# Shift and scale of the first two channel tiles loaded tile by tile, and squares summed on TensorE, in the first projection of a hybrid block

## The chip, the cores and the metric

The kernel runs on one core of a Trainium2 chip. The metric is device microseconds (us) of one execution; a time is the median of several runs. The engines are TensorE (PE, with PEld for its weight loads), VectorE (DVE), ScalarE (ACT), GpSimd (POOL) and SyncE (SP), which here issues nearly all loads.

## The reference, cut to what matters

One layer of a diffusion backbone: a latent stream x of 512 tokens and a context stream of 256 tokens, both 2048 channels wide. The change lies in the first steps, up to the projection of the first heads:

```python
mod = (c_act @ w_mod + b_mod)[:, None, :]          # c_act = silu(c)
mod_c = (cc_act @ w_mod + b_mod)[None, None, :]
sh1, sc1, gt1, sh2, sc2, gt2 = jnp.split(mod, 6, axis=-1)
csh1, csc1, cgt1, csh2, csc2, cgt2 = jnp.split(mod_c, 6, axis=-1)
h = rmsnorm(x, g_norm1) * (1 + sc1) + sh1
hc = rmsnorm(ctx, g_norm1) * (1 + csc1) + csh1
lat_in, lat_gates = project_heads(h, w_in, gla_w_lr, gla_b_lr, mlstm_b_gate)
ctx_in, ctx_gates = project_heads(hc, w_in, gla_w_lr, gla_b_lr, mlstm_b_gate)
...
x = x + gt1 * merge_groups(lat_gla, lat_ml, lat_gates[0], lat_gates[1],
                           gla_g_norm, mlstm_g_norm, w_out, x.dtype)
h2 = rmsnorm(x, g_norm2) * (1 + sc2) + sh2
x = x + gt2 * conv_ffn(h2, rows, GRID_W, w_up, conv_w, conv_b, w_down)
```

Everything is float32. Behind the projection come two scans in both directions, an output projection, an MLP with a 3x3 convolution and a last norm.

## The kernel before, in words

Activations stand transposed: a channel tile is 128 channels by 512 latent tokens (`xl[k]`, 16 tiles, 256 KB each) or by 256 context tokens (`xc[k]`, loaded in pairs). Products of the layer split both operands into a high part of type fp32r and a low part and sum three matmuls (`mm3`): ScalarE casts the high part (`split`, a CAST), VectorE subtracts it for the low part. The norm's sums and the shift and scale sums run in plain float32.

`project_first` computes the projections of heads 0 and 1 together, as the weights of the adaLN shift and scale still come in. Stage kp covers the two channel tiles 2 kp and 2 kp + 1, with a weight of 512 KB per head (`raw_h`). A head has six groups: two of x with a moving operand of 512 tokens (g = 0, 1), two of x with tokens on the output's partitions (g = 2, 3), two of the context stream (g = 4, 5). Head 0 accumulates over all stages in six PSUM banks (`banks`, tag acc). Head 1 sums each stage in a bank of its own (tag psb, two buffers) and is moved to SBUF (`sums`, tiles `e`), by ScalarE in stage 0 and by an add on VectorE later (`early_group`; `early_pair` does g = 0 and 1 of stage 0 at once).

What stands before the first product: `stream_rstd` squares the 16 x tiles on ScalarE, adds them up on VectorE, sums over channels with one matmul against ones (`ss_l`) and takes the root (`mean_rsqrt`, result `rl`). `mod_load` loads the shift or scale weights of two channel tiles (four tiles `raw_m` of 512 KB), `mod_rows` sums them in 16 matmuls (`ps_m`) and copies them out on ScalarE, `mod_cols` turns them into columns (two small matmuls) that VectorE puts into `scol` (region 1, scale) or `shcol` (region 0, shift). `modulate` multiplies tiles with the root, applies scale and shift, and splits them into `hTh` and `hTl` (x) or `hch` and `hcl` (context). The context stream has its own norm (`ss_c`, `rc`) while the first x products run. Eight matmuls of ones and `rl` without a use of their own precede the first product.

The order on PE is the program's (`pinned`); on the other engines a scheduler sets it from priorities, and `tc.issue_after` and `behind` hold an instruction behind a named one of its engine. Loads go through one queue of SP, in program order; each issue waits for the landing of the load eight places ahead, and for its buffer (`mraw`, seven; `wraw`, four).

Of the kernel before, what the change touches and what calls it, by code (L numbers as in the profile page):

```python
# [18 lines left out]
P = 128  # L19
# [27 lines left out]
C_END = C_ONE + 1  # L47


def constants():  # L50
# [7 lines left out]
    c[:, C_ONE] = 1.0  # L58
    return c
# [11 lines left out]
def block_kernel(ctx: ExitStack, tc: tile.TileContext, a: dict, out: bass.AP):  # L71
# [43 lines left out]
    cols = keep.tile([P, 148], F32, name="cols")  # L115
# [160 lines left out]

    def mod_cols(region, n, bank, rows):

        pc = bank[:, 256:260].rearrange("p (b c) -> p b c", c=2)
        for b in range(2):  # L280
            mm(pc[:, b, :], rows[:, P * b : P * b + P], cc(C_SA, 2), start=True, stop=True)
        with tc.high_priority():
            for b in range(2):
                k = 2 * n + b
                if region == 1:
                    V.tensor_scalar(out=scol[:, k, :], in0=pc[:, b, :], scalar1=bp1[:, k : k + 1],
                                    scalar2=gn1[:, k : k + 1], op0=ALU.add, op1=ALU.mult)
                else:
                    V.tensor_scalar(out=shcol[:, k, :], in0=pc[:, b, :], scalar1=bmod[:, k : k + 1],
                                    scalar2=None, op0=ALU.add)  # L290
# [105 lines left out]
    def early_pair(w, sums):  # L396

        (wh, wl), ps = w, [psb(f"a1_0_{g}", BANKS[g]) for g in range(2)]
        for n, (ws, xs) in enumerate(((wh, hx[0]), (wl, hx[0]), (wh, hx[1]))):
            for k in range(2):  # L400
                for g in range(2):
                    mm(ps[g], ws[:, k, P * g : P * g + P], xs[k], start=(n == 0 and k == 0), stop=(n == 2 and k == 1))
        for g in range(2):
            sums[g] = actp.tile(list(BANKS[g]), F32, name=f"e0_{g}", tag=f"ah{KT - 4 + g}")
            with tc.high_priority():
                S.activation(sums[g], ps[g], AF.Copy, scale=SCALE if g == 0 else 1.0)  # L406

    def project_first():

        banks = [acc(f"a0_{g}", BANKS[g]) for g in range(6)]  # L410
        sums = [None] * 4 + [accp.tile([P, DK + DV], F32, name=f"e0_{4 + j}", tag=f"sum{j}") for j in range(CJ)]
        stream_rstd(xl, rl, "l", T)
        for r in (1, 0):
            mod_cols(r, 0, *mod_rows(r, 0, mod_load(r, 0)))
        w1, w0 = (load_split(a["w_heads"][h, 0], f"h{h}_0") for h in (1, 0))
# [3 lines left out]
        with tc.high_priority():  # L419
# [1023 lines left out]
```

## Time and profile before

| what | value |
|---|---|
| time, median of 3 runs | 2513.3 us (2512.97 to 2513.51) |
| the profiled execution's own time | 2511.87 us |
| its span | 2510.1 us |
| PE busy | 2469.3 us, 98% |
| VectorE, ScalarE busy | 1815.0 us (72%), 1024.0 us (41%) |
| share of PE in the chain that ended last | 85% |
| the stage kp = 0, which the change touches | from the start to the first product of kp = 1 at 55.45 us |
| loads | 385 GB/s in the first fortieth of the span, 415 GB/s from 50 to 60 us |

A row of the timeline gives start, duration, engine, line, operation, output<-inputs, form and count, and in brackets the idle time before it with what ended that. A row of the chain gives start, duration and what the chain ran through. A row of a stretch gives its bounds, its length, each engine's busy time with its instructions, the granted TensorE clock, the DMA engines' share and GB/s. An operation of PE in float32 shows as two records.

### The profile page before, as it was taken

Reading aid. Unit: us, or ns where it says so; the run is one execution under the profiler, and the core shown is the slowest. Engines: PE = TensorE matmul, PEld = TensorE weight load, DVE = VectorE, ACT = ScalarE, POOL = GpSimd, SP = SyncE. Lnnn points to the kernel's source line nnn. Section 1 sums busy time; section 2 is a strip of 40 time slices with the busy share of each in tenths; the row PEclk is TensorE's granted clock in tenths of the full one; section 3 lists DMA queues with packets and bytes.
Section 4 is the critical chain, followed back from the end, with each engine's and each line's share of the span. In section 5 each row is a group of like instructions: output and inputs, shape, how many; then the busy total and the mean of one; then the engine's idle time right before and its main releaser. Section 6 shows DMA issues by size and latency. Waiting matters only on the chain.

```text
span 2510.1 us, 39398 instructions
## 1 busy us (share of the span) xinstructions
PE 2469.3 (98%) x15740; PEld 2204.1 (88%) x15740; DVE 1815.0 (72%) x2880; ACT 1024.0 (41%) x1517; POOL 182.5 (7%) x242
## 2 busy tenths in 40 slices
PE   6999999999999999999999999999999999999998
PEld 4887889888987888888989999999999999999997
DVE  6666754554445877858988787878787878787886
ACT  4224543332213233226454444444444444444445
POOL 0000000000000000000020101010101010101022
PEclk9999999999999999999999999999999999999999
DMA  9741011123334878842373737373636363646464
GB/s 385 271 172 42 26 43 51 51 76 125 110 117 155 286 274 304 299 158 99 108 176 101 168 104 166 107 168 104 167 104 166 107 162 108 161 113 160 113 186 135
DMA packets 121552, 372.20 MB, mean 148 GB/s; under 512 B 13908, under 2 KB 18328, under 8 KB 121368
## 3 DMA queue, kind: packets, MB, share of 16 engines
q1 hardware_dynamic: 94680, 318.29, 37.7%
q0 software_dynamic: 25600, 50.34, 11.4%
q8 instruction: 123, 2.02, 0.3%
q10 hardware_dynamic: 1088, 1.05, 0.1%
q14 instruction: 61, 0.50, 0.1%
HBM read 319.30 MB, written 50.33 MB: 147 GB/s over the span
## 4 chain that ended last, share of the span: by engine, by line
PE 85%; issue 9%; DVE 2%; DMA 2%; POOL 1%; ACT 1%; SPq 0%; DVEq 0%; POOLq 0%; ACTq 0%
PE a L98 19%; PE dn L98 17%; PE uv L98 15%; PE ug L98 14%; PE ga L98 7%; PE po L98 4%; PE wo L98 3%; PE sl L98 1%; PE ps_m L98 1%; DMA raw_m<-in_w_mod 1%; PE cst L98 1%; PE s L98 1%; DMA xl<-in_xT 0%; POOL x2d L1269 0%; DMA x2d<-st 0%
## 5 line engine op out<-in xcount | busy, mean ns | idle before, releaser
L98 PE MATMUL dn<-gh,lo_d 128*128 128x512 f32 x672 | 262.3, 390 | 0.3 <-DVE lo_d L93 0.3
L98 PE MATMUL dn<-gh,hi_d 128*128 128x512 f32 x672 | 261.6, 389 | 0.0
L98 PE MATMUL dn<-gl,hi_d 128*128 128x512 f32 x672 | 261.6, 389 | 0.0
L1215 DVE SCALAR_TENSOR_TENSOR cv<-pads,cwt,cv 128x512 f32<-128x512 f32 x344 | 239.5, 748 | 0.6
L1269 POOL DMA_DIRECT2D x2d<-st x160 | 140.1, 928 | 1142.7 <-ACT st L1268 1057.5
L313 DVE SCALAR_TENSOR_TENSOR sum_m<-raw_m,csil,sum_m 128x512 f32<-128x512 f32 x240 | 180.1, 750 | 9.0 <-DMA raw_m<-in_w_mod 3.1
L93 DVE TENSOR_TENSOR lo_buv<-sum_uv,hi_buv 128x1024 fp32r<-128x1024 f32 x80 | 98.0, 1224 | 103.6 <-ACT hi_buv L92 103.6
L98 PEld LDWEIGHTS dn<-gh,lo_d 128*128 128x128 f32 x672 | 126.1, 188 | 28.9 <-DVE lo_d L93 2.6
L98 PE MATMUL a<-hi_h,hTh 128*128 128x256 f32 x512 | 150.4, 294 | 0.5 <-ACT e L406 0.5
L98 PEld LDWEIGHTS dn<-gl,hi_d 128*128 128x128 f32 x672 | 126.2, 188 | 25.9
L98 PEld LDWEIGHTS dn<-gh,hi_d 128*128 128x128 f32 x672 | 126.2, 188 | 25.6
L98 PE MATMUL a<-hi_h,hTl 128*128 128x256 f32 x512 | 144.7, 283 | 0.0
L98 PE MATMUL a<-lo_h,hTh 128*128 128x256 f32 x512 | 144.7, 283 | 0.0
L92 ACT CAST hi_d<-raw_d 128x1024 fp32r<-128x1024 f32 x86 | 88.6, 1030 | 131.9 <-PE ug L98 70.6
L93 DVE TENSOR_TENSOR lo_d<-raw_d,hi_d 128x1024 fp32r<-128x1024 f32 x86 | 102.9, 1196 | 48.1 <-ACT hi_d L92 47.5
L98 PE MATMUL ug<-bth,hi_bug 128*128 128x256 f32 x480 | 136.7, 285 | 0.1
L98 PE MATMUL uv<-bth,lo_buv 128*128 128x256 f32 x480 | 135.9, 283 | 0.8 <-DVE lo_buv L93 0.8
L98 PE MATMUL uv<-bqh,lo_auv 128*128 128x256 f32 x480 | 135.9, 283 | 0.0
L98 PE MATMUL uv<-bth,hi_buv 128*128 128x256 f32 x480 | 135.9, 283 | 0.0
L98 PE MATMUL uv<-bql,hi_auv 128*128 128x256 f32 x480 | 135.8, 283 | 0.0
L98 PE MATMUL ug<-bqh,lo_aug 128*128 128x256 f32 x480 | 135.8, 283 | 0.0
L98 PE MATMUL uv<-btl,hi_buv 128*128 128x256 f32 x480 | 135.8, 283 | 0.0
(379 smaller groups left out, 7347.2 us busy)
## 6 DMA issues: line engine op xcount, KB each, us to landing
raw_m<-in_w_mod SPq DMA_DIRECT2D x192, 512.0 KB, 5.2
raw_d<-in_w_down SPq DMA_DIRECT2D x82, 512.0 KB, 3.4
raw_ug<-in_w_up SPq DMA_DIRECT2D x80, 512.0 KB, 3.5
x2d<-st POOLq DMA_DIRECT2D x160, 256.0 KB, 5.5
raw_uv<-in_w_up SPq DMA_DIRECT2D x80, 512.0 KB, 6.2
raw_h<-in_w_heads SPq DMA_DIRECT2D x64, 512.0 KB, 3.6
raw_ga<-in_w_gates SPq DMA_DIRECT2D x32, 512.0 KB, 4.5
raw_wo<-in_w_out SPq DMA_DIRECT2D x32, 512.0 KB, 4.8
```

The lines of the kernel that those rows point to most:

```text
L92: cast[0] = S.copy(hi, x).ins
L93: return V.tensor_tensor(out=lo, in0=x, in1=hi.bitcast(F32), op=ALU.subtract).ins
L98: ins = PE.matmul(*args, **kw)
L313: V.scalar_tensor_tensor(out=parts[0], in0=x, scalar=ck, in1=parts[0], op0=ALU.mult, op1=ALU.add)
L1215: V.scalar_tensor_tensor(out=t3, in0=src, scalar=w, in1=t3, op0=ALU.mult, op1=ALU.add)
L1269: nc.gpsimd.dma_start(x2d[k], t, accum_op=ALU.add)
```

## The change

Four things change, all in the stage kp = 0 and a little of kp = 1.

- The small inputs `cols` and `cvec` become columns of `consts` and come with it in one load instead of three.
- The squares of x are no longer added in one chain: each goes into a tile of its own, VectorE adds pairs, and eight matmuls sum the pairs on PE. Of the context's squares VectorE now computes every other one, the adds stay.
- Shift and scale of tiles 0 and 1 are loaded tile by tile (`mod_half_load`, two loads of 512 KB for a tile and a region; the host's layout of `w_mod1` follows), summed (`mod_half_rows`, 16 matmuls of 128 columns) and applied tile by tile. The order of loads is: head weight 1, tile 0's four, head weight 0, tile 1's four, then context and the next shift and scale as before.
- `first_groups` multiplies tile 0 into six banks (head 1's g = 0 to 3, head 0's g = 0 and 1), then tile 1 into the same. Head 1's four banks are moved out together; head 0's g = 2 and 3 follow, then `ss_c`, the scale of tiles 2 and 3, the context groups, and the shift of tiles 2 and 3. Tile 4's and 5's scale and shift move from stage 0 into stage 1.

```diff
-    cols = keep.tile([P, 148], F32, name="cols")
+    cols, cv = cst[:, C_COLS:C_CV], cst[:, C_CV:]
...
-    def early_pair(w, sums):
...
+    def mod_half_load(region, b):
+
+        raws = []
+        for q in range(2):
+            raws.append((wraw if b and q else mraw).tile([P, 4, 256], F32, name=f"raw_mh{region}_{b}_{q}", tag="raw"))
+            nc.sync.dma_start(raws[q], a["w_mod1"][8 * region, 2 * b + q])
+        return [raw.rearrange("p a (c n) -> p (a c) n", n=P) for raw in raws]
+
+    def mod_half_rows(region, b, raws):
+
+        bank = psb(f"ps_mh{region}_{b}")
+        for q in range(2):
+            for g in range(8):
+                r = 32 * (g % 4)
+                mm(bank[r : r + 32, 0:P], cact[:, 8 * q + g, :], raws[q][:, g, :], start=(q == 0 and g < 4),
+                   stop=(q == 1 and g >= 4), skip_group_check=True)
+        rows = tmp.tile([P, 256], F32, name=f"rows_mh{region}_{b}", tag="rows")[:, 0:P]
+        with tc.high_priority():
+            S.copy(rows, bank[:, 0:P])
+        return bank, rows
+
+    def mod_half_cols(region, k, bank, rows):
+
+        pc = bank[:, 256:258]
+        mm(pc, rows, cc(C_SA, 2), start=True, stop=True)
+        with tc.high_priority():
+            mod_col(region, k, pc)
+
+    def first_groups(kk, accs, w, x, gs, ends):
+
+        (wh, wl) = w
+        for n, (ws, xs) in enumerate(((wh, x[0]), (wl, x[0]), (wh, x[1]))):
+            first, last = kk == 0 and n == 0, ends and kk == 1 and n == 2
+            for o, g in zip(accs, gs):
+                if g < 2:
+                    mm(o, ws[:, kk, P * g : P * g + P], xs[kk], start=first, stop=last)
+                    continue
+                for b in range(2):
+                    js = slice(P * (2 * g - 4 + b), P * (2 * g - 3 + b))
+                    mm(o[:, b, :], xs[kk][:, js], ws[:, kk, 256:], start=first and b == 0, stop=last,
+                       skip_group_check=True)
 
     def project_first():
 
-        banks = [acc(f"a0_{g}", BANKS[g]) for g in range(6)]
         sums = [None] * 4 + [accp.tile([P, DK + DV], F32, name=f"e0_{4 + j}", tag=f"sum{j}") for j in range(CJ)]
         stream_rstd(xl, rl, "l", T)
-        for r in (1, 0):
-            mod_cols(r, 0, *mod_rows(r, 0, mod_load(r, 0)))
-        w1, w0 = (load_split(a["w_heads"][h, 0], f"h{h}_0") for h in (1, 0))
+        w1 = load_split(a["w_heads"][1, 0], "h1_0")
+        halves = [{r: mod_half_load(r, 0) for r in (1, 0)}]
+        raw0 = load_raw(a["w_heads"][0, 0], "h0_0")
+        halves.append({r: mod_half_load(r, 1) for r in (1, 0)})
         for j in range(KT // 2):
             nc.sync.dma_start(xcp[j], a["ctxT"][j])
         raws = {r: mod_load(r, 1) for r in (1, 0)}
-        with tc.high_priority():
-            ins = modulate(0, "x")
-
-        for _ in range(8):
-            mm(banks[5][:, 0:P], ones, rl[:, 0:P], start=True, stop=True)
-        early_pair(w1, sums)
-        for g in range(2, 4):
-            early_group(0, g, w1, sums)
-        project_chunk(0, *w0, banks[0], 0)
+        early = [acc(f"a1_0_{g}", BANKS[g]) for g in range(4)]
+        banks = [acc(f"a0_{g}", BANKS[g]) for g in range(2)]
+        for k in range(2):
+            rows = {r: mod_half_rows(r, k, halves[k][r]) for r in (1, 0)}
+            for r in (1, 0):
+                mod_half_cols(r, k, *rows[r])
+            with tc.high_priority():
+                ins = modulate((k,), "x")
+                if k == 0:
+                    with behind((ins, cast[0])):
+                        w0 = split_new(raw0, "h0_0", (2, 512))
+            for _ in range(4):
+                if k == 0:
+                    mm(banks[1][:, 0:P], ones, rl[:, 0:P], start=True, stop=True)
+            first_groups(k, early, w1, hx, range(4), True)
+            first_groups(k, banks, w0, hx, range(2), False)
+        for g in range(4):
+            sums[g] = actp.tile(list(BANKS[g]), F32, name=f"e0_{g}", tag=f"ah{KT - 4 + g}")
+            with tc.high_priority():
+                S.activation(sums[g], early[g], AF.Copy, scale=SCALE if g == 0 else 1.0)
+        last = cast[0]
+        banks += [acc(f"a0_{g}", BANKS[g]) for g in range(2, 6)]
+        with tc.high_priority(), behind((ins, last)):
+            stream_rstd([x.rearrange("p a b -> p (a b)") for x in xcp], rc, "c", TC, lambda: (
+                project_chunk(0, *w0, banks[2], 2), project_chunk(0, *w0, banks[3], 3)))
+            ins = modulate((0, 1), "c")
         rows = mod_rows(1, 1, raws[1])
-        project_chunk(0, *w0, banks[1], 1)
         mod_cols(1, 1, *rows)
-        with tc.high_priority(), tc.issue_after(ins):
-            stream_rstd([x.rearrange("p a b -> p (a b)") for x in xcp], rc, "c", TC)
-            ins = modulate(0, "c")
-        for g in range(2, 4):
-            project_chunk(0, *w0, banks[g], g)
+        early_group(0, 4, w1, sums)
+        early_group(0, 5, w1, sums)
         rows = mod_rows(0, 1, raws[0])
-        early_group(0, 4, w1, sums)
+        project_chunk(0, *w0, banks[4], 4)
         mod_cols(0, 1, *rows)
-        early_group(0, 5, w1, sums)
         with tc.issue_after(ins):
-            modulate(1, "xc")
-        w1 = load_split(a["w_heads"][1, 1], f"h1_1")
+            modulate((2, 3), "xc")
+        w1 = load_split(a["w_heads"][1, 1], "h1_1")
         for r in (1, 0):
             raws[r] = mod_load(r, 2)
         nc.sync.dma_start(cst[:, 0:C_SA], a["consts"][:, 0:C_SA])
-        project_chunk(0, *w0, banks[4], 4)
-        rows = mod_rows(1, 2, raws[1])
         project_chunk(0, *w0, banks[5], 5)
-        mod_cols(1, 2, *rows)
         for kp in range(1, KP):
             for g in range(6):
-                if g == 5 and kp + 1 < KP:
+                if g == 3 and kp == 1:
+                    rows = mod_rows(1, 2, raws[1])
+                if g == 5 and 1 < kp < KP - 1:
                     rows = mod_rows(0, kp + 1, raws[0])
                 ins = early_group(kp, g, w1, sums)
                 if g == 2:
                     with tc.issue_after(ins):
                         w0 = load_split(a["w_heads"][0, kp], f"h0_{kp}")
-                    if kp + 2 < KP:
-                        raws[1] = mod_load(1, kp + 2)
-            if kp + 1 < KP:
-                mod_cols(0, kp + 1, *rows)
-                with tc.issue_after(ins):
-                    modulate(kp + 1, "xc")
+                if g == (3 if kp == 1 else 2) and kp + 2 < KP:
+                    raws[1] = mod_load(1, kp + 2)
+            if kp == 1:
+                mod_cols(1, 2, *rows)
             for g in range(6):
+                if g == 1 and kp == 1:
+                    rows = mod_rows(0, 2, raws[0])
+                if g == (2 if kp == 1 else 0) and kp + 1 < KP:
+                    mod_cols(0, kp + 1, *rows)
+                    with tc.issue_after(ins):
+                        modulate((2 * kp + 2, 2 * kp + 3), "xc")
                 if g == 3 and kp + 2 < KP:
                     rows = mod_rows(1, kp + 2, raws[1])
                 project_chunk(kp, *w0, banks[g], g)
...
-    cv = xp.tile([P, 32], F32, name="cv")
-    nc.sync.dma_start(cv, a["cvec"])
     nc.sync.dma_start(cst[:, C_SA:], a["consts"][:, C_SA:])
-    nc.sync.dma_start(cols, a["cols"])
...
-    def stream_rstd(xs, o, name, n):
-
-        tot = xp.tile([P, T], F32, name=f"sq_{name}", tag="sqs")
-        for k, x in enumerate(xs):
-            sq = tot if k == 0 else tmp.tile([P, T], F32, name=f"sq_{name}{k}", tag="sq")
-            S.activation(sq, x, AF.Square)
-            if k:
-                add(tot, tot, sq)
+    def stream_rstd(xs, o, name, n, meanwhile=None):
+
         ps = psb(f"ss_{name}", (P, n))
-        for i in range(0, T, n):
-            mm(ps, ones, tot[:, i : i + n], start=(i == 0), stop=(i + n == T))
+        if n == T:
+            spare = [f"ah{k}" for k in range(2, 12)] + [f"al{k}" for k in range(2, 8)]
+            sqs = []
+            for k, x in enumerate(xs):
+                sqs.append(actp.tile([P, T], F32, name=f"sq_{name}{k}", tag=spare[k]))
+                S.activation(sqs[k], x, AF.Square)
+                if k % 2:
+                    add(sqs[k], sqs[k], sqs[k - 1])
+                    mm(ps, ones, sqs[k], start=(k == 1), stop=(k == KT - 1))
+        else:
+            tot = xp.tile([P, T], F32, name=f"sq_{name}", tag="sqs")
+            for k, x in enumerate(xs):
+                sq = tot if k == 0 else tmp.tile([P, T], F32, name=f"sq_{name}{k}", tag="sq")
+                if k % 2:
+                    S.activation(sq, x, AF.Square)
+                else:
+                    mul(sq, x, x)
+                if k:
+                    add(tot, tot, sq)
+            meanwhile()
+            for i in range(0, T, n):
+                mm(ps, ones, tot[:, i : i + n], start=(i == 0), stop=(i + n == T))
         var = tmp.tile([P, n], F32, name=f"var_{name}", tag="sq")
         scr = tmp.tile([P, n], F32, name=f"scr_{name}", tag="sq")
         mean_rsqrt(ps, D, var, scr, o)
 
     rl, rc = rstd[:, 0:T], rstd[:, T:]
 
-    def modulate(n, streams):
-        for k in (2 * n, 2 * n + 1):
+    def modulate(ks, streams):
+        for k in ks:
             if "x" in streams:
                 mul(xl[k], xl[k], rl)
             if "c" in streams:
                 mul(xc[k], xc[k], rc)
-        for k in (2 * n, 2 * n + 1):
+        for k in ks:
             if "x" in streams:
                 V.tensor_scalar(out=xl[k], in0=xl[k], scalar1=scol[:, k, 0:1],
                                 scalar2=shcol[:, k, 0:1], op0=ALU.mult, op1=ALU.add)
...
-    r["w_mod1"] = w_mod[0][:, : 2 * D].reshape(4, 4, P, 16, 256).transpose(3, 0, 2, 1, 4)
+    r["w_mod1"] = w_mod[0][:, : 2 * D].reshape(4, 4, P, 16, 256).transpose(3, 0, 2, 1, 4).copy()
+    for region in range(2):
+        cols = w_mod[0][:, D * region : D * region + 256].reshape(2, 8, P, 2, P)
+        r["w_mod1"][8 * region] = cols.transpose(3, 0, 2, 1, 4).reshape(4, P, 4, 256)
```

Where PE comes from the first tile to the second (first `a_0_0` and `a_0_1` are head 1's banks, `hTh` and `hTl` the parts of x, `hi_h` and `lo_h` of the weight), before:

```order
L98 MATMUL ps_m_0_278<-cst,rows_m_0_295 128x2 x2
L98 MATMUL a_5_179<-rstd,cst 128x128 x8
L98 MATMUL a_0_0_357<-hTh_340,hi_h_0_303 128x512
L98 MATMUL a_0_1_358<-hTh_340,hi_h_0_303 128x512
L98 MATMUL a_0_0_357<-hTh_345,hi_h_0_303 128x512
L98 MATMUL a_0_1_358<-hTh_345,hi_h_0_303 128x512
L98 MATMUL a_0_0_357<-hTh_340,lo_h_0_304 128x512
L98 MATMUL a_0_1_358<-hTh_340,lo_h_0_304 128x512
```

and now on PE, from tile 0's last products (`a_0_281` and `a_1_282` are banks of head 0) to tile 1's first:

```order
L102 MATMUL a_0_281<-hTl_328,hi_h_0_331 128x512
L102 MATMUL a_1_282<-hTl_328,hi_h_0_331 128x512
L102 MATMUL ps_mh_1_363<-raw_mh_1_0_245,cact 32x128 x8
L102 MATMUL ps_mh_1_363<-raw_mh_1_1_247,cact 32x128 x8
L102 MATMUL ps_mh_1_382<-raw_mh_1_0_249,cact 32x128 x8
L102 MATMUL ps_mh_1_382<-raw_mh_1_1_251,cact 32x128 x8
L102 MATMUL ps_mh_1_363<-cst,rows_mh_1_380 128x2
L102 MATMUL ps_mh_1_382<-cst,rows_mh_1_399 128x2
L102 MATMUL a_0_0_277<-hTh_407,hi_h_0_231 128x512
L102 MATMUL a_0_1_278<-hTh_407,hi_h_0_231 128x512
```

Before, a bank takes one tile behind the other; now the half sums of tile 1 (`ps_mh_1`) stand between all six banks of tile 0 and the first of tile 1.

On PE around the context's sum (`a_1`, `a_2`, `a_3` are banks of head 0, `a_0_4` is head 1's first context group), before:

```order
L98 MATMUL a_1_175<-hTh_345,lo_h_0_310 128x512
L98 MATMUL ps_m_1_411<-cst,rows_m_1_428 128x2 x2
L98 MATMUL ss_c<-sq_c,cst 128x256 x2
L98 MATMUL a_2_176<-hi_h_0_309,hTh_340 128x256
L98 MATMUL a_2_176<-lo_h_0_310,hTh_340 128x256
```

and now on PE, from the end of the last x group to the first context group:

```order
L102 MATMUL a_3_444<-lo_h_0_332,hTh_407 128x256
L102 MATMUL a_3_444<-hi_h_0_331,hTl_408 128x256
L102 MATMUL ss_c<-sq_c,cst 128x256 x2
L102 MATMUL ps_m_1_517<-raw_m_1_0_261,cact 32x256 x4
L102 MATMUL ps_m_1_517<-raw_m_1_1_263,cact 32x256 x4
L102 MATMUL ps_m_1_517<-raw_m_1_2_265,cact 32x256 x4
L102 MATMUL ps_m_1_517<-raw_m_1_3_267,cact 32x256 x4
L102 MATMUL ps_m_1_517<-cst,rows_m_1_534 128x2 x2
L102 MATMUL a_0_4_540<-hi_h_0_231,hch_508 128x384
```

The sum moved from ahead of two x groups to behind them, and the scale sums `ps_m_1` of tiles 2 and 3 from ahead of it to right behind, with the context group after them.

On ScalarE, the squares of the context (`sq_c`) and the moves of head 1's banks (`e_0` to `e_3`), before:

```order
L533 ACTIVATE sq_c_442<-xc_142 128x512
L533 ACTIVATE sq_c_445<-xc_143 128x512
L406 ACTIVATE e_0_371<-a_0_0_357 128x512
L406 ACTIVATE e_1_373<-a_0_1_358 128x512
L533 ACTIVATE sq_c_448<-xc_144 128x512
L533 ACTIVATE sq_c_451<-xc_145 128x512
L392 ACTIVATE e_2_388<-a_0_2_375 128x512
L533 ACTIVATE sq_c_454<-xc_146 128x512
L533 ACTIVATE sq_c_457<-xc_147 128x512
L392 ACTIVATE e_3_403<-a_0_3_390 128x512
L533 ACTIVATE sq_c_460<-xc_148 128x512
```

and now on ScalarE, from tile 1's high part to the root of the context's sum:

```order
L96 CAST hTh_407<-xl_122 128x512
L593 ACTIVATE sq_c_450<-xc_138 128x512
L474 ACTIVATE e_0_435<-a_0_0_277 128x512
L474 ACTIVATE e_1_437<-a_0_1_278 128x512
L474 ACTIVATE e_2_439<-a_0_2_279 128x512
L474 ACTIVATE e_3_441<-a_0_3_280 128x512
L593 ACTIVATE sq_c_456<-xc_140 128x512
L593 ACTIVATE sq_c_462<-xc_142 128x512
L593 ACTIVATE sq_c_468<-xc_144 128x512
L162 ACTIVATE scr_c<-ss_c,eps 128x256
```

Before, squares and moves alternate; now one square stands ahead of the four moves, and three behind. The other four are on VectorE, behind the low part of tile 1.

More of the change, by code (lines that the diff above doesn't have):

```diff
@@ L46, with constants @@
 C_ONE = C_SA + 32
-C_END = C_ONE + 1
-def constants():
+C_COLS = C_ONE + 1
+C_CV = C_COLS + 148
+C_END = C_CV + 32
+def constants(cols, cvec):
     c = np.zeros((P, C_END), np.float32)
@@ L58, in constants @@
     c[:, C_ONE] = 1.0
+    c[:, C_COLS:C_CV] = cols
+    c[:, C_CV:] = cvec
     return c
@@ L275, in mod_rows, with mod_col @@
         return bank, rows
+    def mod_col(region, k, pc):
+        if region == 1:
+            V.tensor_scalar(out=scol[:, k, :], in0=pc, scalar1=bp1[:, k : k + 1],
+                            scalar2=gn1[:, k : k + 1], op0=ALU.add, op1=ALU.mult)
+        else:
+            V.tensor_scalar(out=shcol[:, k, :], in0=pc, scalar1=bmod[:, k : k + 1], scalar2=None, op0=ALU.add)
     def mod_cols(region, n, bank, rows):
@@ L283, in mod_cols @@
             for b in range(2):
[L284 to L290, printed above, removed]
+                mod_col(region, 2 * n + b, pc[:, b, :])
     def mod_tile(name):
@@ L394, in early_group @@
                 return V.scalar_tensor_tensor(out=o, in0=ps, scalar=scale, in1=old, op0=ALU.mult, op1=ALU.add).ins
-    def early_pair(w, sums):
[L398 to L404, printed above, removed]
-            with tc.high_priority():
-                S.activation(sums[g], ps[g], AF.Copy, scale=SCALE if g == 0 else 1.0)
+    def mod_half_load(region, b):
[4 more added lines that the diff above has]
+        return [raw.rearrange("p a (c n) -> p (a c) n", n=P) for raw in raws]
```

9 lines of the change are left out of this document (4 added, 5 removed).

## The prediction

> **What bounds the kernel now.** I read the page first, then the busy time in stretches, then the chain of waits of the first 160 us.
>
> ```profile
> span 2510.1 us, 39398 instructions
> PE 2469.3 (98%) x15740; PEld 2204.1 (88%) x15740; DVE 1815.0 (72%) x2880; ACT 1024.0 (41%) x1517; POOL 182.5 (7%) x242
> 0.00:30.00 30.00, 9.86 (x89) 5.48 (x90) 18.57 (x37) 15.22 (x25) 0.21 (x4) 1.00 0.93 352
> 50.00:60.00 10.00, 10.00 (x81) 8.31 (x81) 6.62 (x15) 4.57 (x8) 0.00 (x0) 1.00 1.03 415
> 14.80 8.89 DMA raw_m<-in_w_mod
> 31.23 8.42 DMA raw_m<-in_w_mod
> ```
>
> TensorE (PE) is busy 98% of the span, and what it lacks lies mostly in the first 30 us (9.86 busy, and none of that a product of the layer). From 50 us on it has no gaps. The chain that ended last runs over loads until 39.65 (31.23 + 8.42) and over PE behind that. So the change, which touches this stage alone, is worth exactly what it moves the point from which PE runs without a wait. I follow PE to the end of the first group of kp = 1, the first place that both kernels pass with the same work still ahead, but for one set of shift and scale sums.
>
> **The loads.**
>
> ```profile
> 0.82 0.39 SPq L509 DMA_DIRECT2D cv<-in_cvec  x1
> 2.20 9.02 SPq L516 DMA_DIRECT2D xl<-in_xT  x16
> 11.58 0.33 SPq L261 DMA_DIRECT2D raw_m<-in_w_mod  x1
> 12.22 4.17 SPq L261 DMA_DIRECT2D raw_m<-in_w_mod  x7
> 19.90 9.07 SPq L417 DMA_DIRECT2D xc<-in_ctxT  x8
> ```
>
> From the ninth on, an issue on SP waits for the landing of the load eight places ahead, so these rows are landings: the last x tile at 12.22 + 4.17 - 0.33 = 16.06, the second head weight at 19.90 + 9.07 - 0.33 = 28.64. Ten loads of 512 KB lie between: 1.26 each. The change issues one small load instead of three, so x begins right behind the first issue, 0.94 earlier; I move all landings by that (between 0 and 0.94, as the rate is the DMA's own; the rows lie next to the upper end). By the new order: x complete 15.1, head weight 16.4, shift and scale of tile 0 complete four loads later at 21.4 (before: eight, 26.2), second head weight 22.7, tile 1's at 27.7.
>
> **From x to the first product.**
>
> ```profile
> 9.65 9.45 DVE L87 TENSOR_TENSOR sq_l<-sq_l,sq_l 128x512 f32<-128x512 f32 x12 [0.32 <-ACT sq_l L533]
> 17.54 0.63 ACT L533 ACTIVATE sq_l<-xl 128x512 f32<-128x512 f32 x1 [0.17 <-DVE sq_l L87]
> 19.15 2.07 PE L98 MATMUL ss_l<-sq_l,cst 128*128 128x512 f32 x2 [19.15 <-DVE sq_l L87]
> 42.25 0.97 PE ss_c L98 x4
> 21.26 0.69 ACT L158 ACTIVATE scr_l<-ss_l,eps 128x512 f32<-128x512 f32 x1 [3.09 <-PE ss_l L98]
> 24.10 0.69 DVE L163 SCALAR_TENSOR_TENSOR rstd<-scr_l,rstd 128x512 f32<-128x512 f32 x1
> 25.58 0.28 DVE L286 TENSOR_SCALAR scol<-ps_m,bp,cols 128x2 f32<-128x2 f32 x1
> 28.81 1.00 DVE L553 TENSOR_SCALAR xl<-xl,scol,shcol 128x512 f32<-128x512 f32 x2
> 29.38 1.14 ACT L92 CAST hTh<-xl 128x512 fp32r<-128x512 f32 x2 [0.66 <-DVE xl L553]
> 29.72 1.22 DVE L93 TENSOR_TENSOR lo_h<-raw_h,hi_h 128x1024 fp32r<-128x1024 f32 x1
> 30.08 1.22 PE L98 MATMUL a<-hTh,hi_h 128*128 128x512 f32 x4
> ```
>
> Before, the adds run in one chain to 19.10 and a single matmul sums them to 21.2. Now ScalarE squares each tile by itself, VectorE adds pairs, and PE takes eight such matmuls. A 512-column f32 sum cost 2.07 as PE's first work and 0.97 (the same columns in two halves) later on; a pair arrives each 1.3. At 0.97 PE keeps up: 15.1 + 0.63 + 0.69 + 0.97, with handovers 17.6. The root took 21.26 to 24.79, 3.5; the weight's low part now stands in it on VectorE (1.22, of which about 0.4 sticks out): 21.6. Two multiplications by the root (0.7 each), one scale and one shift column, 0.54 for the tile, 0.62 for the cast: first product at 24.8, against 30.08. So the start gains 5.3.
>
> **The products on tile 0 and tile 1.**
>
> ```profile
> 65.85 4.30 PE a L98 x24
> 43.22 2.87 PE a L98 x24
> 25.40 1.93 PE L98 MATMUL ps_m<-raw_m,cact 128*32 128x256 f32 x32
> 25.40 1.45 PEld L98 LDWEIGHTS ps_m<-raw_m,cact 128*32 128x32 f32 x32
> ```
>
> Three x groups of two tiles take 4.30; six banks of one tile are the same: 24.8 to 29.1. Now PE comes to tile 1's shift and scale sums, all landed (27.7). Each has as many matmuls as one of 1.93 with half the columns: between 0.97 (half of it) and 1.45 (its weight loads, as many as before); I take 1.0, as PE's time went with the columns, so 31.1 for two. Behind them stands tile 1 itself, and no other product is queued ahead of it. Before, from the end of such sums (27.33) to the first product (30.08) it was 2.75; with one tile instead of two, 0.5 less: 2.2. PE idles, and tile 1 begins at 33.3, its six banks end at 37.6, banks 2 and 3 (2.87) at 40.5.
>
> **The context stream.**
>
> ```profile
> 36.49 2.29 DVE L87 TENSOR_TENSOR sq_c<-sq_c,sq_c 128x512 f32<-128x512 f32 x3 [0.22 <-ACT sq_c L533]
> 32.96 1.09 ACT L406 ACTIVATE e<-a 128x512 f32<-128x512 f32 x2
> 42.36 0.47 DVE L286 TENSOR_SCALAR scol<-ps_m,bp,cols 128x2 f32<-128x2 f32 x2 [3.59 <-PE ps_m L98]
> 46.72 0.73 ACT L92 CAST hch<-xc 128x256 fp32r<-128x256 f32 x2 [2.54 <-DVE xc L559]
> 49.78 2.35 PE a L98 x12
> 52.13 1.86 PE ps_m L98 x32
> 55.25 0.34 PE ps_m L98 x4
> 55.45 0.48 PE L98 MATMUL a<-hTh,hi_h 128*128 128x512 f32 x1
> 51.20 0.68 DVE L93 TENSOR_TENSOR hTl<-xl,hTh 128x512 fp32r<-128x512 f32 x1
> ```
>
> Before, its eight squares and seven adds (0.76 each) were done under products at 38.8. Now four squares move to VectorE, and all eleven operations stand there behind tile 1's low part; ScalarE's second square also stands behind four evictions. Counted from tile 1's start: the first bank is complete at +2.15, four evictions of 0.55 end at +4.35, the square at +5.0, and six VectorE operations that follow, 0.76 each, at +9.6. So the sum is there at 42.9; PE has waited 2.4. With 0.97 it ends at 43.9 (before: 43.22). From there to the first cast's end took 3.86 (47.08); the scale columns of tiles 2 and 3 now stand ahead of the modulation (0.47): 4.3, so context products begin at 48.2. Meanwhile PE has the sums for those columns (1.86 and 0.34) and waits another 2; before, two x groups and a second set filled this time.
>
> Then two context groups (2.2 by the row of 2.35, which has a start-up in it), the shift sums (1.86), a group (1.1), columns (0.34): 53.7, and one last group to 54.8. Here the shift columns lead into tile 2 with only that group as cover: 0.35, 0.54, 0.62 and handovers, 55.4. The first group of kp = 1 then waits inside for the low parts: tile 2's stands behind three modulations (56.3), tile 3's behind one more small one and itself (57.4), and the group ends at 57.9. Before it began at 55.45 and ended at 56.9. One set of sums and columns (2.2), which PE had done by then, is still ahead: 57.9 + 2.2 - 56.9 = 3.2 later. Behind that, every load has time: the last of tiles 4 and 5 is issued as its buffers come free at 46 to 52, some 9 ahead of use; the next scale's four, on SP one group later than before, near 62 for a use near 72.
>
> Added to the profiled run (2511.87: span 2510.1 and 1.77 around it) that is 2515.1; the median of the runs shown is 1.43 above that run, so **2516.5**. A measurement of this kernel tells about 0.2%, 5.0 us, from no change; 3.2 is within.
>
> **The rivals.** *PE starts cold.*
>
> ```profile
> 21.16 3.21 PE L98 MATMUL ps_m<-raw_m,cact 128*32 128x256 f32 x32
> ```
>
> The same sums took 3.21 at 21.16 and 1.93 at 25.40, and ss_l 2.07 against 0.97, though the granted clock stands at 1.00 in the first 30 us: a half-speed state that the clock column doesn't show and that ended after some 4 us of PE work. The change leaves PE in scattered pieces between 17.6 and 24.8 (four sums of 0.4 to 0.7, the columns, four of the eight filler matmuls). If these leave it at half speed, 3.4 us of the work on tile 0 costs double, and everything behind shifts by 1.7 to 2: with the sums at 1.45 in place of 1.0 as well, 3.2 + 1.9 + 0.9 = 6.0, time 2519.3; alone, 2518.4. [...] For it: tile 0's loads come 1.26 apart with idle time between. Against: the columns and fillers lie within 2.5 us of the first product. Chance 0.15, about two thirds of it slower by over 0.2%.
>
> [...]
>
> *The context chain is not late.* If sum and root are there when PE arrives, the waits of 2.4 and 2 go: 3.2 - 4.4 = -1.2, time 2512.1, and with the waits in kp = 1 gone too (0.6 and 1.1) -2.9, 2510.4: faster. It decides from a sum ready at 40.5. For it: the context loads have landed at 32.8, and VectorE has little to do from 27 to 31. Against: the order of instructions puts the squares behind tile 1 on both engines. Chance 0.23.
>
> *The loads don't come earlier.* If the small loads never held x up, tile 0 shifts by 0.9: 2517.4; part of the forecast's own range.
>
> **How the numbers follow.** The sum holds with 0.62, the cold start has 0.15, the early context chain 0.23. The forecast is the first. The range runs from the early chain's end, 2510.4, to the cold start alone plus a little, 2518.6. Faster by over 0.2% would need more than all the waits found behind the first product: 0.02. Slower by over 0.2%: two thirds of 0.15, and little of the sum's own tail: 0.11. The rest, 0.87, lies within.
>
> **What would show it.** Right: the first product near 24.8, a PE gap of some 2 ahead of tile 1, two more of about 2 on either side of ss_c, a wait for hTl in the first group of kp = 1 ending near 57.9, then the old pattern. Wrong: ss_c with no wait ahead of it (early chain), tile 0's six banks taking over 6 in place of 4.3 (cold), or a first product after 27, which would mean that eight sums at 2.07 overran the loads.

## The result, and the profile after

The changed kernel takes 2525.07 us (median of five runs, 2521.27 to 2526.92) against 2513.3 on the same chip (2512.52 to 2515.84): a ratio of 1.0047, 95% interval 1.0033 to 1.0061. It is 11.8 us slower, where 3.2 were forecast, and lies outside the range. The head of the page after:

```profile
span 2525.2 us, 39493 instructions
PE 2484.9 (98%) x15810; PEld 2213.1 (88%) x15810; DVE 1813.9 (72%) x2877; ACT 1022.3 (40%) x1515; POOL 183.0 (7%) x242
```

TensorE's rows from the timeline after (start, duration, in brackets the idle time before and what ended it; rows between them left out):

```profile
25.21 0.74 PE L102 MATMUL a<-hTh,hi_h 128*128 128x512 f32 x2 [0.55 <-ACT hTh L96]
29.61 1.95 PE L102 MATMUL ps_mh<-raw_mh,cact 128*32 128x128 f32 x64
33.93 0.79 PE L102 MATMUL a<-hTh,hi_h 128*128 128x512 f32 x2 [1.54 <-ACT hTh L96]
34.52 1.05 PE L102 MATMUL a<-hi_h,hTh 128*128 128x256 f32 x4
38.39 0.62 PE L102 MATMUL a<-hTh,hi_h 128*128 128x512 f32 x2
44.84 2.05 PE L102 MATMUL ss_c<-sq_c,cst 128*128 128x256 f32 x4 [2.03 <-DVE sq_c L91]
46.81 2.55 PE L102 MATMUL ps_m<-raw_m,cact 128*32 128x256 f32 x32
51.86 0.69 PE L102 MATMUL a<-hi_h,hch 128*128 128x384 f32 x1 [1.39 <-ACT hch L96]
60.69 0.50 PE L102 MATMUL a<-hTh,hi_h 128*128 128x512 f32 x1 [0.45 <-ACT hTh L96]
70.16 0.44 PE L102 MATMUL a<-hi_h,hch 128*128 128x384 f32 x1 [0.78 <-DVE e L400]
72.13 0.44 PE L102 MATMUL a<-hi_h,hch 128*128 128x384 f32 x1 [0.65 <-DVE e L400]
75.61 0.50 PE L102 MATMUL a<-hTh,lo_h 128*128 128x512 f32 x1 [1.25 <-DVE lo_h L97]
```

The first product comes 4.9 us earlier, the waits ahead of tile 1 and of `ss_c` are there, and yet the first group of kp = 1 starts at 60.69 in place of 55.45. Two things were not in the sum. First, equal work takes unequal time: pieces of 1024 columns take 0.62 at 38.39 and 1.05 at 34.52, `ss_c` takes 2.05 where 0.97 was taken over, and sums that took 1.86 take 2.55. Second, kp = 1 has three waits, 2.7 us together (70.16, 72.13, 75.61). Stretches of 3.4 us say what the first one is (busy time of each engine, behind it the granted clock and the loads):

```profile
core 0: us, PE busy (x) PEld busy (x) DVE busy (x) ACT busy (x) POOL busy (x), PEclk, DMA share, GB/s
31.10:34.50 3.40, 1.73 (x26) 1.27 (x15) 1.64 (x4) 1.42 (x3) 0.00 (x0) 0.99 1.06 410
34.50:37.90 3.40, 3.40 (x13) 3.02 (x12) 3.29 (x6) 0.16 (x1) 0.00 (x0) 0.50 1.01 405
37.90:41.30 3.40, 3.40 (x24) 3.13 (x23) 0.91 (x2) 2.64 (x6) 0.00 (x0) 1.00 1.02 407
41.30:44.70 3.40, 1.51 (x13) 1.30 (x11) 3.15 (x5) 1.04 (x2) 0.00 (x0) 1.00 1.03 410
44.70:48.10 3.40, 3.26 (x17) 1.77 (x21) 0.65 (x2) 0.89 (x2) 0.00 (x0) 0.50 0.16 65
48.10:51.50 3.40, 1.87 (x28) 1.01 (x20) 2.73 (x9) 0.47 (x2) 0.00 (x0) 1.00 0.75 251
51.50:54.90 3.40, 3.04 (x9) 3.04 (x10) 2.82 (x7) 1.12 (x3) 0.00 (x0) 0.50 0.90 339
```

Three stretches run at a granted clock of 0.50, each right behind one in which PE was busy 44 to 55% (1.73, 1.51 and 1.87 of 3.40), none of them empty. Before, the stretches from 30 to 60 us are all at 1.00.

For the comparisons below I use two instructions that every kernel runs: the first product of kp = 1 ("the start of kp = 1", 55.45 before), and the first of a later group of the same stage (68.56 before, behind the moved set of scale sums). The offset of a kernel is its start there less that of before; it is free of what the rest of the program does in one execution. The changed kernel stands at +5.2 and +11.9, and the latter stays within 1.2 until 2498 us; the spans of the two profiles differ by 15.1, so the last 2 us of that arise at the very end, in work that the change doesn't touch. So the 11.9 that arise ahead of 81 us are about the 11.8 of the median.

### The profile page after: what moved, and what is told of

Its sections match the earlier page's. It is cut to its first block, busy times and chain, and to the rows that moved or that the text cites. A ratio compares the mean times of both kernels' runs of the same rounds, so it can differ in the third digit from the quotient of the medians.

```text
span 2525.2 us, 39493 instructions
## 1 busy us (share of the span) xinstructions
PE 2484.9 (98%) x15810; PEld 2213.1 (88%) x15810; DVE 1813.9 (72%) x2877; ACT 1022.3 (40%) x1515; POOL 183.0 (7%) x242
## 3 DMA queue, kind: packets, MB, share of 16 engines
q8 instruction: 124, 2.03, 0.3%
q10 hardware_dynamic: 1088, 1.05, 0.1%
## 4 chain that ended last, share of the span: by engine, by line
PE 84%; issue 9%; DVE 3%; DMA 2%; ACT 1%; POOL 0%; SPq 0%; DVEq 0%; POOLq 0%; ACTq 0%
PE a L102 19%; PE uv L102 16%; PE dn L102 15%; PE ug L102 14%; PE ga L102 7%; PE po L102 4%; PE wo L102 3%; PE sl L102 1%; PE ps_m L102 1%; DVE cv L1277 1%; DMA raw_uv<-in_w_up 1%; PE cst L102 1%; DVE lo_d L97 1%; PE s L102 1%; DMA xl<-in_xT 0%
```

## The experiments

**Fillers where the clock fell.**

```diff
+    def idle(bank, n):
+        for _ in range(n):
+            mm(bank[:, 0:P], ones, rl[:, 0:P], start=True, stop=True)
...
+            if k == 1:
+                idle(psb("idle_1", (P, P)), 6)     # behind tile 1's columns
...
-    project_chunk(0, *w0, banks[2], 2), project_chunk(0, *w0, banks[3], 3)))
+    project_chunk(0, *w0, banks[2], 2), project_chunk(0, *w0, banks[3], 3), idle(banks[4], 8)))
...
         mod_cols(1, 1, *rows)
+        idle(banks[5], 7)
```

> The changed kernel with filler matmuls (ones by the root, 128 columns) in three places where PE waits in stage 0: six ahead of tile 1, eight ahead of ss_c, seven ahead of the first context group. Theory A (PE falls to half speed because it works too little in three windows of 3.4 us): the three stretches at a granted clock of 0.5 between 34 and 55 us go, the first group of kp = 1 starts some 4 to 5 us earlier than at 60.7, the time falls to about 2520. Rival B (the waits alone cost the time, the clock follows and costs little): the clock column goes to 1.00, but the group starts within 1 us of 60.7 and the time stays at 2524 to 2526.

2520.64 us, ratio to before 1.002 (1.0011 to 1.0029): 4.4 less than the changed kernel, by work that only fills waits.

```profile
30.00:40.00 10.00, 9.79 (x109) 8.80 (x98) 6.14 (x11) 4.78 (x10) 0.00 (x0) 1.00 1.02 390
40.00:50.00 10.00, 9.20 (x86) 7.48 (x86) 7.75 (x19) 2.73 (x7) 0.00 (x0) 1.00 0.95 379
50.00:60.00 10.00, 9.31 (x69) 6.71 (x68) 6.95 (x16) 4.14 (x8) 0.00 (x0) 1.00 0.87 311
```

```profile
43.15 1.13 PE L102 MATMUL ss_c<-sq_c,cst 128*128 128x256 f32 x4 [0.31 <-DVE sq_c L91]
48.66 0.42 PE L102 MATMUL a<-hi_h,hch 128*128 128x384 f32 x1
56.18 0.50 PE L102 MATMUL a<-hTh,hi_h 128*128 128x512 f32 x1 [0.46 <-ACT hTh L96]
```

First the stretches from 30 to 60 us of this kernel, then three rows of its timeline: the clock is 1.00 throughout, and the path is the predicted one (context sum done near 43.9: here 44.3; context products 48.2: 48.66; kp = 1 at 55.4: 56.18). The offset is +0.7 at the start of kp = 1 and +7.4 at the second mark. So 4.5 of the 11.9 are the half clock, 0.7 are left at the start of kp = 1, and 6.7 arise within it. The 4.5 belong to the first profile of the changed kernel: two more executions of the same stage 0, shown below, start kp = 1 at +3.4 (the kernel with the earlier scale columns) and +4.5 (the repeat), 2.6 and 3.8 over this kernel. The median of the fillers' eleven runs, 4.4 lower and with no overlap of the intervals, agrees in size.

**The scale sums' bank in kp = 1.** The changed kernel sums the next scale ahead of g = 3 and makes its columns behind g = 5. Until then the sums hold one of the two psb buffers, and head 1's g = 3 to 5 share the other.

```diff
+                if g == 4 and kp == 1:
+                    mod_cols(1, 2, *rows)
                 ins = early_group(kp, g, w1, sums)
...
-            if kp == 1:
-                mod_cols(1, 2, *rows)
...
-                    with tc.issue_after(ins):
+                    with tc.issue_after(ins), tc.issue_after(parted[0]):
                         modulate((2 * kp + 2, 2 * kp + 3), "xc")
```

> The changed kernel with the scale columns of tiles 4 and 5 computed after the fourth group of kp = 1 instead of the sixth, so that their PSUM bank is free two groups sooner. Theory A: the waits of PE for the moves of e (0.8 and 0.7 at 70 and 72 us) go, the wait for the head weight's low part (1.2 at 75.6) stays in part; the time falls by 1.5 to 2.5, to about 2523. Rival C (no bank is short, VectorE is simply late): the waits stay, the time stays within 0.5 of the changed kernel.

2524.78 us, 1.0038 (1.0026 to 1.0051). The wait at 72.13 goes, that at 70.16 falls from 0.78 to 0.44, but the long one stays, 1.32: `lo_h` still stands behind head 1's last add on VectorE. The growth within kp = 1 falls from 6.7 to 5.4, and the median by only 0.3, which five runs can't tell from nothing. A half success in the trace; the time alone decides nothing.

**Both, and the weight's low part ahead of the last add.** The fillers and the earlier columns, and in kp = 1

```diff
+                with tc.issue_after(parted[0]) if kp == 1 and g == 5 else nullcontext():
                     ins = early_group(kp, g, w1, sums)
```

> Fillers and the earlier scale columns together, and the head weight's low part in kp = 1 ahead of the sixth move on VectorE, as it stood before the change. Theory A: both gains add up, with 1 more for the low part: about 2517, which is the 3 us over the kernel before that the prediction's waits add up to. If the two share a cause, the gain is that of the larger one alone: 2520.

2518.65 us, 1.0014 (1.0005 to 1.0023): 2.0 less than with fillers alone, between the two expectations. The waits of kp = 1 in this kernel's timeline:

```profile
66.24 0.44 PE L102 MATMUL a<-hi_h,hch 128*128 128x384 f32 x1 [0.44 <-DVE e L400]
69.33 0.50 PE L102 MATMUL a<-hTh,lo_h 128*128 128x512 f32 x1 [0.28 <-DVE lo_h L97]
```

And in that of the kernel with fillers alone:

```profile
65.66 0.44 PE L102 MATMUL a<-hi_h,hch 128*128 128x384 f32 x1 [0.78 <-DVE e L400]
67.62 0.44 PE L102 MATMUL a<-hi_h,hch 128*128 128x384 f32 x1 [0.65 <-DVE e L400]
71.11 0.50 PE L102 MATMUL a<-hTh,lo_h 128*128 128x512 f32 x1 [1.25 <-DVE lo_h L97]
```

0.7 us in place of 2.7, and the growth within kp = 1 is 4.3 in place of 6.7: 2.4 are the bank and the low part behind it. What is left is 3.8 over before in the median, close to the 3.2 that the prediction found in waits and moved sums. The profile doesn't bear this closeness out: its offset at the second mark is 5.6, of which 1.3 stand at the start of kp = 1, and it works at half pace from 23.04 to 26.6 us (eight records of the four matmuls on the root 1.88 in place of 1.14, the first two products 1.22 in place of 0.73, both against fillers alone), in the work on tile 0, where no filler was added.

**The context's root earlier.** From there: two context squares on VectorE ahead of tile 1's work, the others on ScalarE right behind tile 1's high part, the matmuls for their sum between banks 2 and 3.

```diff
+                    with behind((parted[0], cast[0])):
+                        ctx_squares((0, 1), (0, 1))
...
+            ctx_squares((7, 2, 3, 4, 5, 6), (7,))
+            project_chunk(0, *w0, banks[2], 2)
+            ctx_root(lambda: project_chunk(0, *w0, banks[3], 3))
```

> The version with both repairs (fillers and the earlier scale columns of channel tile 2), with the context's squares moved: two squares on VectorE ahead of tile 1's work, the others on ScalarE right behind tile 1's high part, the matmuls for their sum between banks 2 and 3 of tile 0's left operand, tile 1's context sums behind one early group. Theory A, that the 3.8 us left over before are the wait for the context's root mean square that the change put late: ss_c's matmuls start at 40 to 41 us in place of 43 to 44, context products near 45, the first group of kp=1 near 52 us; 2514 to 2516 us, 3 to 4 less than the version with both repairs and within 0.1% of before. Rival: that chain isn't what is left, and the time stays within 0.7 of that version.

2517.06 us, 1.001 (1.0001 to 1.0019): 1.6 less, on another chip, where 3 to 4 were expected; the two intervals overlap, so the time alone doesn't tell it from nothing. In the trace the chain does move:

```profile
39.85 1.10 PE L102 MATMUL ss_c<-sq_c,cst 128*128 128x256 f32 x4 [0.41 <-DVE sq_c L91]
44.89 0.44 PE L102 MATMUL a<-hi_h,hch 128*128 128x384 f32 x1
53.41 0.50 PE L102 MATMUL a<-hTh,hi_h 128*128 128x512 f32 x1 [0.72 <-ACT hi_h L96]
54.67 0.50 PE L102 MATMUL a<-hTh,lo_h 128*128 128x512 f32 x1 [0.53 <-DVE lo_h L97]
```

kp = 1 starts 2.0 ahead of before, and 2.8 behind at the second mark: a new wait for kp = 1's head weight (0.72 and 0.53) and the set of sums still ahead eat the lead. It has the lowest median of the variants of the change, and is not better than before.

**One filler place alone.** Six fillers behind tile 1's columns and no other edit.

> The changed kernel with six filler matmuls at one place only, behind the columns of channel tile 1. Theory A, each half-speed stretch by its own price: the one at 34.5 us is gone, those near 44.7 and 51.5 stay, tile 1's first part takes 0.63 per piece in place of 1.05, and the time falls by 1 to 2 us against the changed kernel. Rival, that only the stretch that ends last counts, since work waits behind the context's root anyway: the stretch is gone and the time stays within 0.4.

2523.43 us, 1.0036 (1.0024 to 1.0049): 1.6 less than the changed kernel, which the overlap of the two intervals doesn't tell from nothing, and 1.5 in the trace at the second mark. Tile 1's pieces take 0.63, and the half clock further on stays (0.83 over 40 to 50 and over 50 to 60 us). But the fillers needn't be the reason. The kernel with the earlier scale columns has no filler here, and between 17 and 60 us its timeline has half pace only at `ss_c` and the sums behind it (2.05 at 42.94, 2.55 at 44.91) and in the context products from 49.97 on (0.52, later 0.33); in it tile 1's pieces take 0.63 too:

```profile
34.47 0.63 PE L102 MATMUL a<-hTh,lo_h 128*128 128x512 f32 x2
```

And the profile with the fillers has half speed where the first one didn't have it, in the work on tile 0: the clock is 0.83 over 20 to 30 us, and the first two products take 1.22 in place of 0.74. So this run doesn't settle what one stretch costs.

**The parts without the tile-by-tile loads.** Before, with the single small load and x's squares summed by eight matmuls:

```diff
-    nc.sync.dma_start(cv, a["cvec"])
...
-    nc.sync.dma_start(cols, a["cols"])
...
+                if k % 2:
+                    add(sqs[k], sqs[k], sqs[k - 1])
+                    mm(ps, ones, sqs[k], start=(k == 1), stop=(k == KT - 1))
```

> The kernel before with two parts of the change alone: the small inputs in one load, and the squares of x summed by eight matmuls over pairs. Order of loads, products and the rest as before. Theory A (the first product waits for the shift weights at 26.2, not for the root): the root is there 3 us earlier and the first product comes 0.5 to 1 earlier than at 30.08; the time falls by 0 to 1. Rival D (the eight matmuls delay the shift and scale sums on PE, or PE is cold for them): 1 to 3 slower.

2518.15 us, 1.0011 (1.0002 to 1.002): 3.3 slower, as the rival had it (1 to 3), and not faster. From 12.6 us on its sums take 1.12 in place of 2.07, so PE is at full pace early. While tile 0's shift and scale come in, PE is busy 63% of a stretch (20.7 to 24.1 us); the clock is 0.50 from there on for 6.8 us (a quarter of the sums takes 1.08 at 24.25, 0.64 at 22.98), and the first product comes at 31.18 in place of 30.08. The offset is 0.7 at both marks, so in this profile the start explains under 1 us. The same with two filler matmuls behind each quarter of tile 0's and 1's shift and scale sums:

```diff
+                for _ in range(2):
+                    mm(spare[:, 0:P], ones, ones, start=True, stop=True)
```

> The kernel of the e4_sum run (before with the small inputs in one load and the squares of x summed on TensorE) with two filler matmuls behind each quarter of the first two modulation tiles' sums. Theory A, that e4_sum was slower by its 6.8 us at half speed from 24.1 us on: no half-speed stretch between 11 and 60 us, first product at 29.5 to 30.1 us in place of 31.18, 2514 to 2515.5 us, 2.5 to 4 less than e4_sum. Rival, that the half speed there was not what cost: within 0.7 of e4_sum.

2516.52 us, 1.0007 (0.9998 to 1.0016). The clock is 1.00 from 10 to 90 and from 210 to 230 us, first product at 29.93 (rows of its timeline below), offset +0.2 at both marks and 0.0 near 2500 us. The time is 1.6 less than without fillers, between the two expectations, and the two intervals overlap; the trace agrees with the first. The earlier root buys nothing here: in the kernel without fillers `ps_m` waits five times for its loads, 2.1 us in all, and with the fillers the first product comes only 0.15 earlier than before.

```profile
27.67 0.61 PE L102 MATMUL ps_m<-cst,rows_m 128*128 128x2 f32 x4
28.14 2.03 PE L102 MATMUL a<-rstd,cst 128*128 128x128 f32 x16
29.93 1.22 PE L102 MATMUL a<-hTh,hi_h 128*128 128x512 f32 x4
```

**Before without its fillers.**

```diff
-        for _ in range(8):
-            mm(banks[5][:, 0:P], ones, rl[:, 0:P], start=True, stop=True)
```

> The kernel before without its eight filler matmuls ahead of the first product. Theory A, that a stretch of some 3.4 us in which TensorE is about half busy is enough for half speed: the first products then run at half speed, a stretch of 3.4 us or more behind 30 us, and the time grows by 1.5 to 2 us. Rival, that only a stretch without any work lowers the clock: no half-speed stretch there, and the time moves by at most 0.3.

2514.52 us, 1.0001 (0.9992 to 1.0009). Its stretches:

```profile
26.10:29.50 3.40, 1.35 (x20) 0.74 (x12) 1.95 (x7) 2.03 (x4) 0.00 (x0) 1.00 1.03 407
29.50:32.90 3.40, 3.34 (x8) 2.67 (x9) 3.40 (x5) 3.04 (x6) 0.00 (x0) 0.50 1.05 406
```

The half clock is there, as theory A has it, behind a stretch with 1.35 of 3.40 busy; its price is not: the products start at 29.56, without fillers ahead of them, and the offset is 0.65. The time agrees with the rival, the clock with theory A: these fillers cost nearly what they save.

**The same kernels once more**, for what is the program's and what the execution's. The changed kernel:

> The changed kernel once more, unaltered, for its granted clock. Theory A: the clock is set for stretches of 3.413 us on a grid that starts at another point in each execution, by how busy TensorE was in the stretch before; so the half-speed stretches below 60 us stand at other times than 34.5, 44.7 and 51.5 us, in steps of 3.413 us among themselves, two to four of them, each behind a stretch in which TensorE was busy under about 0.6, and none behind one over 0.75. Rival: the gate answers to the gaps of the program themselves, and the stretches come at 34.5, 44.7 and 51.5 us again, within 0.3.

```profile
20.10:23.50 3.40, 2.18 (x39) 1.66 (x40) 3.19 (x7) 0.49 (x2) 0.00 (x0) 1.00 1.03 411
23.50:26.90 3.40, 3.40 (x15) 2.97 (x14) 2.42 (x4) 1.56 (x2) 0.00 (x0) 0.50 1.03 408
40.60:44.00 3.40, 1.22 (x11) 1.04 (x10) 3.02 (x5) 0.91 (x2) 0.00 (x0) 1.00 1.04 410
44.00:47.40 3.40, 3.39 (x20) 1.88 (x24) 0.78 (x2) 0.89 (x2) 0.00 (x0) 0.50 0.44 177
47.40:50.80 3.40, 1.80 (x28) 0.95 (x20) 2.66 (x9) 0.54 (x2) 0.00 (x0) 1.00 0.75 269
50.80:54.20 3.40, 3.11 (x10) 3.11 (x11) 2.76 (x7) 1.05 (x3) 0.00 (x0) 0.50 0.90 277
```

And the first products on tile 0 in this execution:

```profile
24.85 1.22 PE L102 MATMUL a<-hTh,hi_h 128*128 128x512 f32 x2
```

2525.54 us, offset +11.2 at the second mark. The stretch at 34.5 is gone, and one at 23.5 has come, in the work on tile 0, whose first two products take 1.22 in place of 0.74 and which takes 5.3 us in place of 4.4; it stands behind one with 2.18 of 3.40 busy, a little more than the expected 0.6. The distances are multiples of 3.413, the length of a half-speed stretch in the first execution's trace (23.5 to 44.0: six, 44.0 to 50.8: two), as they are there (34.5, 44.7, 51.5: three and two). But the last two stand 0.7 earlier here, while tile 1's first product stands 0.56 later (34.49 against 33.93). So in these two executions the half-speed stretches don't stand at fixed places of the program, and the same wait is followed by half speed in one and not in the other: PE waits 1.54 ahead of tile 1 in both, and tile 1's second piece takes 1.05 in the first and 0.65 here.

The kernel with the small load and the sums by matmuls:

> The kernel of the e4_sum run once more, unaltered. Theory A: its half-speed stretch at 24.1 us and its 9.6 us at the end of the profile hang on where the grid stood and on that execution, so that the offset against before is again 0 to 1 at 80 us, while the growth between 1150 and 2150 us isn't there again in that size (below 4). Rival, that the program causes that growth: 8 to 10 at the end again.

2518.16 us (one run). The growth of the offset from 1100 us to the end, 8.9 in its first profile, is 2.2 here: the larger part belongs to the execution, and its cause is open. The offset at 80 us is 2.5, where 0 to 1 was expected: half speed goes on into the first products, which take 2.05 at 31.93, where the first profile has 1.17 at 31.18.

## Why the prediction was wrong

- **The start** held: first product 25.21 (24.8), tile 0 done at 29.6 (29.1), two half sums in 1.95 (2.0), tile 1 at 33.93 (33.3). Eight matmuls for x's sum kept up with the loads: the last began at 17.25, after a wait of 0.22 for VectorE's pair, and took 1.12.
- **The context chain** held: PE waited 2.03 (2.4) for the sum, and with a full clock the products came at 48.66 (48.2) and kp = 1 at 56.18 (55.4), 0.8 late. The rival of an early chain was wrong.
- **The clock is the first step that failed.** "PE starts cold" looked for half speed at one place of four, behind the pieces from 17.6 to 24.8 ahead of tile 0, and it got 0.15. There it came in three of the seven profiles of the kernels with the change (first two products on tile 0 in 1.22 in place of 0.74: with both repairs, with one filler place, in the repeat), not in the first; in the repeat it cost 0.9 (5.3 against 4.4), half of the 1.7 to 2 that the rival gave it. No row that the prediction shows gives the 3.4 us that the rival let cost double; where half speed came behind the three waits, it lasted 3.40 in the rows after. The sum took durations at full clock everywhere behind 24.8, although it had itself found three waits there of 2.2, 2.4 and 2 us. In the first profile each of these waits has a half-speed stretch behind it, 4.5 us together (against the run with fillers); in the other two executions of this stage without fillers only the last two of the three waits have one. What goes ahead of half speed is in the rows after and of the repeat a stretch with 1.22 to 2.18 of 3.40 busy, with no wait in it over 2.19 (ahead of `ss_c` in the repeat).
- **kp = 1 is the second.** "Then the old pattern" was assumed behind the first group. But the moved scale sums brought their bank along: one of two psb buffers held over three groups, and VectorE's `lo_h` behind the columns and the add. 2.4 us of this were taken out again (both repairs against fillers alone), and about 1 more of the 6.7 that arise there (forecast: 3.2) is not assigned; part of it is that a wait costs more than its row. With fillers alone, the row of 1.25 stands between two starts that are 1.65 apart, and 0.23 before: 1.4 us.
- Together: 3.2 forecast, 4.5 for the clock, 3.4 in kp = 1, 0.8 at its start: 11.9, the offset measured. The 3.2 are the forecast itself and were not measured apart. It is in part luck that one profile's offset and the median (11.8) agree this well: the three executions without fillers start kp = 1 from 3.4 to 5.2 late.

The chance given to slower by over 0.2%, 0.11, came from one place for the cold clock where there were four, and from the kp = 1 stage left out.

## What to carry to other kernels

A start that is brought forward pays only if what follows is brought forward too: here it opened waits of 1.4 to 2.2 us, and two or three of them, by the execution, cost again behind them, as half a clock. Where a sum finds waits on TensorE, give a chance to half speed in the work behind each (here 3.40 us at 0.50 where it came), or fill the wait with matmuls and count what these cost where the engine would not have waited. And when a step moves, list the buffers that it holds while it waits to finish, and who shares them.

## What the runs showed of the hardware

In the traces' record of the granted clock (from 23.78 us on in before, from 13.98 in after), up to 2490 us, each half-speed stretch is 3.413 us long: one in before, at 1143.36, and five in after, at 34.46, 44.70, 51.53, 225.61 and 1157.44, whole multiples of 3.413 apart (the last two 273). In the repeat of the changed kernel they stand at other times, 23.5, 44.0 and 50.8, six and two such lengths apart.

PE was busy in the 3.40 us ahead of half-speed stretches for 1.73, 1.51, 1.87 and, at 222.2, 2.18 (after), 2.18, 1.22 and 1.80 (the repeat), 1.35 (before without its fillers), 1.94 (the kernel with the earlier context root). But in 3.41 us with 1.78 at 218.34 and 2.10 at 447.04 in before, and with 2.11 at 68.59, 2.23 at 72.00 and 2.10 at 461.12 in after, the next stretch stayed at 1.00. And near 1150 us half speed stands behind nearly full stretches, with 3.22 of 3.41 busy at 1154.03 in after; in before:

```profile
1140.00:1143.40 3.40, 3.18 (x26) 2.70 (x25) 3.05 (x4) 2.52 (x4) 1.09 (x2) 0.99 0.59 231
1143.40:1146.80 3.40, 3.40 (x18) 3.40 (x18) 0.65 (x4) 0.47 (x2) 0.00 (x0) 0.50 0.71 236
```

Four other profiles (the kernel with the earlier context root, before without its fillers, the small load and the sums with fillers, one filler place alone) have a clock of 0.91 over 1140 to 1160 us, with PE busy 19.60 to 19.78 of the 20. In the last 30 us the clock is at 0.50 from 2501.86 in before and from 2512.54 in after to the end, behind 3.4 us with 1.47 and 2.89 busy. So busy time did not decide alone in these runs; what else did stays open. Near 215 us before's profile has 2.29 of 3.40 in a stretch and keeps its clock; that of the kernel with the earlier context root has 1.94 and loses it for two stretches, though PE is busy 3.13 of 3.40 in the first of them:

```profile
208.10:211.50 3.40, 2.29 (x16) 1.89 (x16) 1.93 (x3) 2.99 (x7) 0.00 (x0) 1.00 0.00 0
```

```profile
211.40:214.80 3.40, 1.94 (x15) 1.54 (x13) 2.28 (x3) 2.99 (x7) 0.00 (x0) 1.00 0.00 0
214.80:218.20 3.40, 3.13 (x10) 2.91 (x11) 3.28 (x12) 2.22 (x6) 0.00 (x0) 0.51 0.04 9
218.20:221.60 3.40, 3.40 (x14) 3.40 (x14) 2.12 (x9) 1.14 (x2) 0.00 (x0) 0.50 0.00 1
```

Whether the places of these stretches make part of the spread between runs of one kernel (before: 2511.4 to 2520.1 in 27 runs) was not tested.
